# Gate weights of a second feed-forward: high part by a rounding DMA, low part by an accumulating DMA

## The chip, the cores and the metric

One core of one Trainium2 chip runs the whole program. The metric is the device time of one execution in microseconds (us); the kernel before takes 1485.97 us (median of three runs, 1485.88 to 1487.15).

## What is computed

Two layers of a transformer-like backbone over 512 latent and 128 context tokens, width 1024. Layer 0 has neighbourhood attention, layer 1 a bidirectional gated linear recurrence; each is followed by a feed-forward with SwiGLU, inner width 2816, and a final norm closes the network. The change lies in the second feed-forward:

```python
def _swiglu(x, w_gu, w_down):
    gate, up = jnp.split(x @ w_gu, 2, axis=-1)
    return (jax.nn.silu(gate) * up) @ w_down

f_c = _swiglu(_modulate(ctx, norm_g[i, 1], sh2_c, sc2_c), ffn_w_gu[i], ffn_w_down[i])
f_l = _swiglu(_modulate(lat, norm_g[i, 1], sh2_l, sc2_l), ffn_w_gu[i], ffn_w_down[i])
```

All in float32. The gate and up weights of one layer are 1024 x 2816 each.

## The kernel before, in words

Every matmul product is made of three passes in a reduced float32 format (`F32R` in the code): a value is split into a rounded high part and the remainder, the low part, and the product is high x high + high x low + low x high. So each weight tile (128 x 1024, 512 KB) has to become two tiles before TensorE can use it. `split` (L1527 to L1530) does that for a tile in `raw`: ScalarE copies it with rounding into the high part (L1529), VectorE subtracts the high part from `raw` into the low part (L1530).

The 2816 inner features are 22 tiles of 128. The second feed-forward (`ffn_halves`) handles them in chunks of 3, 3, 4, 4, 4 and 4; after each chunk a down projection (`project_part`, at the end `project_last`) adds the chunk's share to the tokens `x`. Tiles 0 to 2 are prepared in `opening`, the function ahead of it. For tiles 3 to 21, one call of `gate_weights` each (19 calls), a scheme with sums of blocks saves matmuls: the gate tile's two halves are the blocks A11 and A12, four sums S1 to S4 of gate and up blocks are formed by GpSimd (`sum_weights`, `s_sums`, L1175) and split in turn (`s_split`), and the second half of the up tile is split by `last_weights`. A tile's products run in three parts: `pair_a` (A11 and A12, L1203 to L1205 in `product`), `pair_b` (S2, S1, S3) and `pair_c` (A22, S4). Only `pair_a` reads the gate tile's high and low part; GpSimd's sums read the unsplit gate tile in `raw` as well.

Buffers: `raw` has three, filled by SP's DMA queue; `whi` and `wlo`, the high and low parts, have three each, shared in turn by the gate tiles and the weights of the down projection. The accumulator bank `mc` is one, reused by each tile. A scheduler in the build sets the order of each engine's instructions from its own estimate of times. Each engine then works strictly in that order, and an instruction that waits holds up all behind it.

The main lines are: in `gate_weights`, the DMA into `raw` (L1156), the two buffers and `self.split(hi, lo, raw)` (L1159).

Of the kernel before, what the change touches and what calls it, by code (L numbers as in the profile page):

```python
# [9 lines left out]
F32 = mybir.dt.float32  # L10
F32R = mybir.dt.float32r
AF = mybir.ActivationFunctionType
ALU = mybir.AluOpType
# [125 lines left out]
class _Step:  # L139
# [66 lines left out]
    def keep(self, todo, n):  # L206
        nc = self.nc
        for _ in range(min(n, len(todo))):
            name, f = key = todo.pop(0)
            raw = self.t([P, D], F32, "mraw", 3, self.sb)  # L210
            if name == "wg":
                nc.gpsimd.dma_start(raw.rearrange("p (f m) -> p f m", f=2), self.i[name][2 * f:2 * f + 2].rearrange("f p w d m -> p f (w d m)"))
            else:
                nc.gpsimd.dma_start(raw.rearrange("p (k m) -> p k m", k=KT), self.i[name][1, f] if name == "gu" else self.i[name][f])
            self.kept[key] = d = self.dram.tile([P, 2 * D], F32, tag=f"k{name}{f}", name=f"k{name}{f}")
            high, low = [self.t([P, D], F32R, n, 1, self.sb) for n in ("kwh", "kwl")]
            with self.tc.issue_after(self.mark[0]), self.tc.issue_after(self.mark[1]):
                nc.scalar.copy(high, raw)  # L218
                nc.vector.tensor_tensor(low, raw, high.bitcast(F32), ALU.subtract)
            for h, w in enumerate((high, low)):  # L220
                nc.gpsimd.dma_start(d[:, h * D:h * D + D], w.bitcast(F32))

    def two(self, src, x):
        nc = self.nc
        n = src.shape[2]
        raw = self.t([P, 2, n, P], F32, "raw", 3)
        nc.sync.dma_start(raw, src.rearrange("f p k m -> p f k m"))
        hi = self.t([P, 2, n, P], F32R, "whx" if x else "whi", 3, self.sb if x else None)
        lo = self.t([P, 2, n, P], F32R, "wlx" if x else "wlo", 3, self.sb if x else None)
        self.split(hi, lo, raw)  # L230
        return [(hi[:, j], lo[:, j]) for j in range(2)]
# [921 lines left out]
    def gate_weights(self, l, f):  # L1153
        nc = self.nc
        raw = self.t([P, KT, P], F32, "raw", 3)
        nc.sync.dma_start(raw, self.i["gu"][l, f])  # L1156
        hi = self.t([P, KT, P], F32R, "whi", 3)
        lo = self.t([P, KT, P], F32R, "wlo", 3)
        self.split(hi, lo, raw)  # L1159
        W = {n: (hi[:, a:a + KH], lo[:, a:a + KH]) for n, a in (("A11", 0), ("A12", KH))}  # L1160
        return {"W": W, "g": raw, "u": self.i["gu"][l, NF + f]}

# [517 lines left out]
```

## Time and profile before

| what | value |
|---|---|
| median of three runs | 1485.97 us (1485.88 to 1487.15) |
| the profiled execution | 1488.96 us, span 1487.1 us |
| TensorE matmul busy | 1471.2 us, 99% of the span |
| VectorE busy | 1075.0 us, 72% |
| ScalarE busy | 728.3 us, 49% |
| GpSimd busy | 247.9 us, 17% |
| second feed-forward, `gate_weights` on | about 1050 to 1480 us |

Engines are named PE (TensorE matmul), PEld (its weight loads), DVE (VectorE), ACT (ScalarE), POOL (GpSimd) and SP (the queue that issues most DMAs). A busy share is an average; what an engine waits for is read from its waits, stretch by stretch. Durations are those of one profiled execution.

### The profile page before, as it was taken

To read this page: it belongs to the slowest core of one execution; us is meant where nothing else is said; L and a number is where in the kernel's file an instruction comes from. 1 tells how busy PE (TensorE), PEld (TensorE's weight loads), DVE (VectorE), ACT (ScalarE), POOL (GpSimd) and SP (SyncE) were. 2 spreads that over 40 slices of the span, in tenths; PEclk is the share of its full clock that TensorE was granted. 3 is DMA by queue.
4 is the path that set the end of the run, shared out by engine and by line. 5 is a ranking of instruction groups with operands and counts; after the bars stand their busy time and mean duration, and the time that the engine had idled before them with its cause. 6 is when DMAs were issued, how large, how long until landed. Compare 5 with 4: busy or idle time off the path is not lost.

```text
span 1487.1 us, 26372 instructions
## 1 busy us (share of the span) xinstructions
PE 1471.2 (99%) x10377; PEld 1440.2 (97%) x10377; DVE 1075.0 (72%) x2054; ACT 728.3 (49%) x1345; POOL 247.9 (17%) x325
## 2 busy tenths in 40 slices
PE   9999999999999999999999999999999999999997
PEld 5999999999999999999999999999999999999997
DVE  6788887875678788887876489985865666565545
ACT  5676666754333234322434298864634343424344
POOL 0001000000012222211210001112032322222311
PEclk9999999999999999999999999999999999999999
DMA  9555555443359899886863744267242131313121
GB/s 371 179 151 172 170 151 155 126 157 100 114 177 323 299 358 326 305 264 218 306 221 125 252 142 142 86 236 247 81 132 86 57 114 57 114 57 109 52 68 71
DMA packets 86026, 255.35 MB, mean 172 GB/s; under 512 B 9056, under 2 KB 22544, under 8 KB 85776
## 3 DMA queue, kind: packets, MB, share of 16 engines
q1 hardware_dynamic: 59152, 157.06, 32.3%
q0 software_dynamic: 26576, 96.49, 18.8%
q8 instruction: 81, 1.33, 0.4%
q14 instruction: 41, 0.34, 0.1%
q10 hardware_dynamic: 176, 0.13, 0.0%
HBM read 206.18 MB, written 43.53 MB: 168 GB/s over the span
## 4 chain that ended last, share of the span: by engine, by line
PE 79%; DMA 8%; DVE 5%; issue 3%; ACT 3%; POOL 1%; DVEq 0%; ACTq 0%; POOLq 0%
PE mm L253 11%; PE mm L255 11%; PE mm L254 11%; PE mx L253 4%; PE mx L255 4%; PE mx L254 4%; PE mx L1203 3%; PE mx L1204 3%; PE mx L1205 3%; DMA mraw<-in_wm 2%; PE op L888 2%; PE gp L1412 2%; PE tp L806 2%; PE mc L1204 1%; PE mc L1203 1%
## 5 line engine op out<-in xcount | busy, mean ns | idle before, releaser
L253 PE MATMUL mm<-big,whi 128*128 128x320 f32 (+3 forms) x1010 | 311.0, 311 | 1.9 <-ACT big L1529 1.8
L254 PE MATMUL mm<-big,whi 128*128 128x320 f32 (+3 forms) x1010 | 312.7, 310 | 0.3 <-DVE big L1530 0.3
L255 PE MATMUL mm<-big,wlo 128*128 128x320 f32 (+3 forms) x1010 | 312.2, 310 | 0.0
L292 DVE SCALAR_TENSOR_TENSOR mprod<-mraw,csb 128x1024 f32<-128x1024 f32 x160 | 194.7, 1217 | 19.6 <-DMA mraw<-in_wm 19.4
L253 PEld LDWEIGHTS mm<-big,whi 128*128 128x128 f32 x1010 | 189.6, 189 | 4.0 <-ACT big L1529 2.4
L254 PEld LDWEIGHTS mm<-big,whi 128*128 128x128 f32 x1010 | 190.5, 189 | 1.7 <-DVE big L1530 0.5
L255 PEld LDWEIGHTS mm<-big,wlo 128*128 128x128 f32 x1010 | 190.1, 189 | 1.0
L1529 ACT CAST whi<-raw 128x1024 fp32r<-128x1024 f32 (+2 forms) x103 | 105.3, 1024 | 143.7 <-PE mm L254 89.6
L1530 DVE TENSOR_TENSOR wlo<-raw,whi 128x1024 fp32r<-128x1024 f32 (+2 forms) x103 | 127.4, 1238 | 33.4 <-ACT whi L1529 33.1
L254 PE MATMUL mm<-big,whx 128*128 128x320 f32 (+3 forms) x443 | 137.4, 310 | 0.0
L255 PE MATMUL mm<-big,wlx 128*128 128x320 f32 (+3 forms) x443 | 137.2, 310 | 0.0
L253 PE MATMUL mm<-big,whx 128*128 128x320 f32 (+3 forms) x443 | 137.0, 310 | 0.0
L595 DVE SCALAR_TENSOR_TENSOR x<-mm,G,x 128x320 f32<-128x320 f32 (+3 forms) x202 | 81.1, 435 | 55.9 <-PE mm L255 50.7
L253 PE MATMUL mx<-big,whi 128*128 128x320 f32 (+3 forms) x318 | 99.2, 312 | 0.0
L255 PE MATMUL mx<-big,wlo 128*128 128x320 f32 (+3 forms) x318 | 98.6, 310 | 0.0
L254 PE MATMUL mx<-big,whi 128*128 128x320 f32 (+3 forms) x318 | 98.4, 310 | 0.0
L288 POOL DMA_DIRECT2D mraw<-in_wm x80 | 42.9, 536 | 317.1 <-DVE mprod L292 203.9
L255 PEld LDWEIGHTS mm<-big,wlx 128*128 128x128 f32 x443 | 83.6, 189 | 0.0
L254 PEld LDWEIGHTS mm<-big,whx 128*128 128x128 f32 x443 | 83.5, 189 | 0.0
L253 PEld LDWEIGHTS mm<-big,whx 128*128 128x128 f32 x443 | 83.4, 188 | 0.0
L1530 DVE TENSOR_TENSOR wlx<-sum,whx 128x1024 fp32r<-128x1024 f32 x40 | 50.2, 1254 | 38.5 <-ACT whx L1529 38.5
L218 ACT CAST kwh<-mraw 128x1024 fp32r<-128x1024 f32 x33 | 34.7, 1051 | 75.6 <-DMA kwi<-kwh 27.7
(396 smaller groups left out, 3886.5 us busy)
## 6 DMA issues: line engine op xcount, KB each, us to landing
raw<-in_gu SPq DMA_DIRECT2D x84, 512.0 KB, 3.6
mraw<-in_wm POOLq DMA_DIRECT2D x80, 512.0 KB, 5.3
raw<-in_dn SPq DMA_DIRECT2D x24, 512.0 KB, 3.7
sw<-in_wm SPq DMA_DIRECT2D x16, 512.0 KB, 10.1
raw<-in_wqk SPq DMA_DIRECT2D x16, 512.0 KB, 4.4
mraw<-in_wi POOLq DMA_DIRECT2D x16, 512.0 KB, 6.4
kwi<-kwh POOLq DMA_DIRECT2D x16, 512.0 KB, 6.3
kwi<-kwl POOLq DMA_DIRECT2D x16, 512.0 KB, 5.4
```

Of the source, the lines that this page charges most:

```text
L218: nc.scalar.copy(high, raw)
L253: nc.tensor.matmul(ps, hi[:, k], xhi[:, k, s], start=(k == 0), stop=False)
L254: nc.tensor.matmul(ps, hi[:, k], xlo[:, k, s], start=False, stop=False)
L255: nc.tensor.matmul(ps, lo[:, k], xhi[:, k, s], start=False, stop=(k == nk - 1))
L288: nc.gpsimd.dma_start(w, self.i["wm"][l * 6 + j - 2, f])
L292: nc.vector.scalar_tensor_tensor(prod, w, 1.0, self.csb[:, s], ALU.mult, ALU.mult, accum_out=out[:, s, f:f + 1])
L595: last = self.nc.vector.scalar_tensor_tensor(xs, ps[:, a - t0:b - t0], G[:, s, f:f + 1], xs, ALU.mult, ALU.add).ins
L1203: nc.tensor.matmul(ps, hi[:, k], xh[:, k], start=start and k == 0, stop=False, skip_group_check=not start)
L1204: nc.tensor.matmul(ps, hi[:, k], xl[:, k], start=False, stop=False, skip_group_check=not start)
L1205: nc.tensor.matmul(ps, lo[:, k], xh[:, k], start=False, stop=(k == KH - 1), skip_group_check=not start)
L1529: high = self.nc.scalar.copy(hi, v).ins
L1530: return high, self.nc.vector.tensor_tensor(lo, v, hi.bitcast(F32), ALU.subtract).ins
```

## The change

A new function `rounded` takes the place of `split` in `gate_weights`. GpSimd's queue loads the gate tile once more from HBM, straight into the high part, rounding on the way; ScalarE writes the negated high part into the low part's buffer; a second GpSimd transfer adds the tile from HBM onto it, which leaves tile minus high part. The load into `raw` stays, since GpSimd's sums read it.

```diff
+    def rounded(self, hi, lo, src):
+        nc = self.nc
+        nc.gpsimd.dma_start(hi, src)
+        nc.scalar.mul(lo, hi.bitcast(F32), -1.0)
+        nc.gpsimd.dma_start(lo, src, accum_op=ALU.add)
...
     def gate_weights(self, l, f):
         nc = self.nc
         raw = self.t([P, KT, P], F32, "raw", 3)
         nc.sync.dma_start(raw, self.i["gu"][l, f])
         hi = self.t([P, KT, P], F32R, "whi", 3)
         lo = self.t([P, KT, P], F32R, "wlo", 3)
-        self.split(hi, lo, raw)
+        self.rounded(hi, lo, self.i["gu"][l, f])
```

Below, lines of the changed kernel are 6 higher than before; the numbers behind names count buffers.

The scheduler moves the work around the new instructions. On GpSimd, at the chunk of tiles 10 to 13, before: the sums of tiles 12 (`sum_14219`, `sum_14220`) and 13 stand in one row (`raw` holds the unsplit tiles).

```order
L1175 TENSOR_TENSOR sum_14219<-raw_14217 128x512
L1175 TENSOR_TENSOR sum_14220<-raw_14180,raw_14217 128x512
L1175 TENSOR_TENSOR sum_14219<-sum_14219,raw_14180 128x512
L1175 TENSOR_TENSOR sum_14220<-raw_14180,sum_14219 128x512
L1175 TENSOR_TENSOR sum_14352<-raw_14350 128x512
L1175 TENSOR_TENSOR sum_14352<-sum_14352,raw_14313 128x512
```

The same place on GpSimd in the changed kernel; the gate tiles 11 to 14 are `whi_14057`, `whi_14191`, `whi_14325` and `whi_14459`, their low parts one number higher.

```order
L1181 TENSOR_TENSOR sum_14230<-raw_14189,raw_14227 128x512
L225 DMA whi_14057<-in_gu 128x1024
L1181 TENSOR_TENSOR sum_14229<-sum_14229,raw_14189 128x512
L1181 TENSOR_TENSOR sum_14230<-raw_14189,sum_14229 128x512
L227 DMA wlo_14058<-in_gu 128x1024
L225 DMA whi_14191<-in_gu 128x1024
L227 DMA wlo_14192<-in_gu 128x1024
L225 DMA whi_14325<-in_gu 128x1024
L225 DMA whi_14459<-in_gu 128x1024
L227 DMA wlo_14326<-in_gu 128x1024
L227 DMA wlo_14460<-in_gu 128x1024
L1181 TENSOR_TENSOR sum_14363<-raw_14361 128x512
```

Between the sums of tile 12 and those of tile 13 now stand eight transfers of four tiles; the accumulate of tile 13 stands behind the load of tile 14.

On ScalarE, at the same chunk, before: the casts of tiles 11, 12 and 13 (`whi_14049`, `whi_14182`, `whi_14315`) and, behind them, that of tile 12's sums (`whx_14225`).

```order
L1529 CAST whi_14049<-raw_14047 128x1024
L1529 CAST whi_14182<-raw_14180 128x1024
L1529 CAST whi_14315<-raw_14313 128x1024
L1209 COPY snap_14066<-mx_14053 128x320
L1216 ACTIVATE g_14081<-g_14081 128x320
L1529 CAST wuh_14133<-raw_14084 128x512
L1529 CAST big_11721<-g_13692 128x320
L1529 CAST whx_14225<-sum_14219 128x1024
```

In the changed kernel (tile 12's sums are `sum_14229` here), the negations stand where the casts stood.

```order
L226 ACTIVATE wlo_14058<-whi_14057 128x1024
L226 ACTIVATE wlo_14192<-whi_14191 128x1024
L1215 COPY snap_14075<-mx_14062 128x320
L226 ACTIVATE wlo_14326<-whi_14325 128x1024
L1222 ACTIVATE g_14090<-g_14090 128x320
L1535 CAST wuh_14142<-raw_14093 128x512
L1535 CAST big_11721<-g_13700 128x320
L1535 CAST whx_14235<-sum_14229 128x1024
```

The negation of tile 13, which waits for a transfer into `whi_14325`, stands four rows ahead of the cast of tile 12's sums.

On TensorE, at tile 4 (`whi_12654`, `wlo_12655`), before: its first products in `pair_a`, and the down projection (`mm`) between them.

```order
L1203 MATMUL mx_12658<-big_11262,whi_12654 128x320
L1204 MATMUL mx_12658<-big_11262,whi_12654 128x320
L1205 MATMUL mx_12658<-big_11262,wlo_12655 128x320
L1203 MATMUL mx_12658<-big_11262,whi_12654 128x320
L1204 MATMUL mx_12658<-big_11262,whi_12654 128x320
```

In the changed kernel (tile 4 is `whi_12655` and `wlo_12656`):

```order
L1209 MATMUL mx_12660<-big_11262,whi_12655 128x320
L1210 MATMUL mx_12660<-big_11262,whi_12655 128x320
L259 MATMUL mm_12546<-big_11721,whi_12508 128x320
L260 MATMUL mm_12546<-big_11722,whi_12508 128x320
L261 MATMUL mm_12546<-big_11721,wlo_12509 128x320
L259 MATMUL mm_12546<-big_11721,whi_12508 128x320
```

The first product with the low part was the third matmul of the tile; now 27 matmuls of the down projection stand between the first two and it.

## Rows read from the trace of the kernel before

**Rows 1.** The page: busy us, share of the span and instructions of each engine.

```profile
PE 1471.2 (99%) x10377; PEld 1440.2 (97%) x10377; DVE 1075.0 (72%) x2054; ACT 728.3 (49%) x1345; POOL 247.9 (17%) x325
```

**Rows 2.** Busy us of each engine (instructions) by stretches, granted clock, DMA share.

```profile
core 0: us, PE busy (x) PEld busy (x) DVE busy (x) ACT busy (x) POOL busy (x), PEclk, DMA share, GB/s
1060.00:1080.00 20.00, 19.48 (x133) 19.22 (x132) 17.78 (x39) 11.47 (x25) 2.29 (x3) 1.00 0.38 124
1080.00:1130.00 50.00, 49.06 (x332) 48.57 (x332) 33.10 (x55) 19.93 (x32) 17.51 (x13) 1.00 0.33 99
1130.00:1180.00 50.00, 49.73 (x336) 49.23 (x335) 32.51 (x56) 19.18 (x30) 14.11 (x11) 1.00 0.31 95
1180.00:1230.00 50.00, 49.65 (x338) 49.38 (x337) 29.06 (x44) 24.16 (x41) 13.95 (x11) 1.00 0.28 85
1230.00:1280.00 50.00, 50.00 (x343) 50.00 (x342) 29.36 (x46) 16.20 (x27) 16.51 (x12) 1.00 0.21 64
1280.00:1330.00 50.00, 50.00 (x342) 50.00 (x341) 29.98 (x50) 17.79 (x26) 11.49 (x9) 1.00 0.32 96
1330.00:1380.00 50.00, 49.90 (x340) 49.64 (x339) 30.34 (x44) 23.14 (x40) 13.78 (x11) 1.00 0.31 95
1380.00:1430.00 50.00, 50.00 (x343) 50.00 (x342) 29.04 (x48) 17.27 (x26) 13.64 (x10) 1.00 0.24 70
1430.00:1487.00 57.00, 48.91 (x334) 47.81 (x332) 31.38 (x63) 25.42 (x51) 4.90 (x6) 0.96 0.17 60
sum 427.00, PE 416.73 PEld 413.84 DVE 262.55 ACT 174.56 POOL 108.17; mean PE 46.30 PEld 45.98 DVE 29.17 ACT 19.40 POOL 12.02
```

**Rows 3.** What TensorE waited for from 1000 us on: us in total, times, longest.

```profile
PE mx L1203 <- ACT snap L1209: 1.4, 3, 0.5
PE at L521 <- ACT snap L665: 0.4, 1, 0.4
PE mm L1203 <- DVE x L595: 0.4, 1, 0.4
PE mm L253 <- ACT big L1529: 0.4, 1, 0.4
PE mx L542 <- DVE dg L538: 0.3, 1, 0.3
```

**Rows 4.** Splitting weight tiles from 1000 us on: count, duration ns min/median/max.

```profile
L1529 ACT CAST whi<-raw x41: 824/1048/1056, 1060.0 to 1431.3; 128x1024 fp32r<-128x1024 f32 x33, 128x768 fp32r<-128x768 f32 x8
L1530 DVE TENSOR_TENSOR wlo<-raw,whi x41: 943/1225/2285, 1061.3 to 1432.4; 128x1024 fp32r<-128x1024 f32 x33, 128x768 fp32r<-128x768 f32 x8
```

**Rows 5.** GpSimd's loads into tile mraw, whole span: issue ns, then landings.

```profile
L288 POOL DMA_DIRECT2D mraw<-in_wm x80: 528/531/727, 45.1 to 752.9; - x80
...
L214 POOL DMA_DIRECT2D mraw<-in_wi x16: 527/536/563, 426.8 to 591.5; - x16
...
DMA to landing us min/median/max: 3.7/5.6/9.6
```

**Rows 6.** SP's queue from 1050 to 1440 us: packets, MB, share of 16 engines.

```profile
q1 hardware_dynamic: 12864, 33.03, 27.7%
```

**Rows 7.** The page: mean busy share of the DMA engines, in 40 slices, tenths.

```profile
DMA  9555555443359899886863744267242131313121
```

**Rows 8.** One of GpSimd's four sums of a tile, from 1050 to 1440 us.

```profile
L1175 POOL TENSOR_TENSOR sum<-raw x19: 1287/1295/1640, 1048.8 to 1414.7; 128x512 f32<-128x512 f32 x19
```

**Rows 9.** What SP's queue waited for from 1050 to 1440 us: total, times, longest.

```profile
SPq L1156 <- DVE wlo L1530: 103.3, 15, 13.7
SPq L227 <- POOL sum L1175: 46.6, 6, 10.3
```

## The prediction

> **What bounds the kernel now.** I read the page's busy line first: the matmul engine is busy 99% of the span, VectorE 72%, GpSimd 17% [rows 1]. That share is an average, so the table by stretches came next, for the second feed-forward's products and the stretch that closes it. TensorE is idle there for 0.52, 0.94, 0.27, 0.35, 0, 0, 0.10 and 0 us between 1060 and 1430 us, 2.2 us in all, at a granted clock of 1.00; VectorE and ScalarE are free a third to two thirds of the time [rows 2]. Last, TensorE's list of waits from 1000 us on: 2.9 us in seven waits, none for a weight tile's high or low part, none for a DMA [rows 3]. So TensorE bounds this stage, and the work that the change takes off VectorE is hidden today. The stretch 1280 to 1330 gives the pace: 342 matmuls in 50.00 us, 0.146 us each [rows 2].
>
> **The change part by part.** *Removed:* 19 gate tiles (feed-forward tiles 3 to 21) lose a subtraction of 1.225 us on VectorE [rows 4], 23.3 us of busy time that no TensorE wait is put down to [rows 3]: on the path 0, at most the 2.2 us above. *Exchanged:* the 19 rounding casts on ScalarE become 19 negations of the same 128x1024. No negation of that size is in the trace; the cast took 1.048 us [rows 4] and I take 1.05. *Added:* 38 transfers of 512 KB on GpSimd's queue. A load takes GpSimd 0.53 us to issue [rows 5]: 38 x 0.53 = 20 us beside its 108 us in 427 [rows 2], which is hidden as work. DMA traffic: the SP queue moved 33.03 MB in 390 us for 27.7% of the engines [rows 6], so 512 KB occupy all sixteen for 0.277 x 390 x 0.524 / 33.03 = 1.7 us. The additions are 19 x (1.7 + 3.4) = 97 us of 390: room enough on average.
>
> What matters is the chain from the release of a weight buffer to the low part's arrival. Before, it was cast and subtraction, 1.05 + 1.23 = 2.3 us [rows 4], on data that already lay in `raw`. Now it is rounding load, negation, accumulating transfer, one after the other. The trace has neither kind of transfer. Plain loads of this size on GpSimd's queue landed in 3.7 us at the least, 5.6 in the median and 9.6 at the most [rows 5]; these are the bounds for both. For the rounding load I take 4.0, near the low end, because the stage's DMA share is 0.21 to 0.38 [rows 2] where most of those loads ran at 5 to 9 tenths [rows 7]. The accumulating one reads the tile twice, from HBM and from its destination, so I give it one share more: 4.0 + 1.7 = 5.7. The Trainium skill says the same in "Collectives: The Full Stack", section "The bandwidth ceiling: the fold count and why AG ≠ RS ≠ AR": an add in the DMA path costs through its two source reads, about half the copy rate; by a plain copy's price the sum below would be near 0, by that rule what it is now. No run here shows it yet. With 0.3 us for three hand-overs (my allowance) the chain is 4.0 + 1.05 + 5.7 + 0.3 = 11.0 us, 8.7 longer than before.
>
> Against it stands the distance, in the changed order, from the last matmul that reads the buffer's previous content to the first that reads the new low part, at 0.146 us a matmul.
> - *Tiles 4, 5, 6* (TensorE rows of the change section): 72, 75 and 79 matmuls, 10.5, 11.0 and 11.5 us. Loads 5 and 6 stand on GpSimd right behind the accumulate of the tile before and share the DMA engines with it; of its two shares I charge one, 1.7 us. Waits 0.5 + 1.7 + 1.2 = 3.4 us.
> - *Tiles 8, 9:* tile 8's accumulate stands on GpSimd behind tile 9's load, which waits for its buffer and behind two sums of 1.3 us [rows 8]; tile 9's first product comes 39 matmuls, 5.7 us, after its buffer is free, and 4.0 + 1.7 are needed before any of that. I charge 3.
> - *Tiles 11 to 21 but the last of each four:* 104 to 107 matmuls, 15.2 us or more, so the low part itself arrives in time. But ScalarE's negation of the third tile (13, 17, 21) waits for a landing at the head of its queue (ScalarE rows): behind it stands the cast of the second tile's sums, behind that on VectorE a subtraction and the gate addition that frees the `mc` bank. From the release of the second tile's buffer to TensorE's product into that bank are 120 matmuls, 17.5 us. The chain: load 4.0 + 1.7, negation 1.05, two issues 1.1, third load behind a whole accumulate 4.0 + 3.4, negation 1.05, cast 1.05, subtraction 1.23, addition 0.5, hand-overs 0.4 = 19.5. So 2.0 us, three times: 6.
> - *The end:* the gate transfers delay GpSimd's sums, the sums free `raw` buffers, and SP's loads for the down projections already wait for such sums, 46.6 us in 6 waits [rows 9]. For the last projection I charge two waits of ScalarE's casts, 3 us.
>
> Sum: 3.4 + 3 + 6 + 3 = 15.4, rounded to 16 because GpSimd's queue also delays what I did not count. Against the profiled execution's own 1488.96 us (span 1487.1 and 1.9 around it) that is 1505; the median of the three runs lies 3.0 below that execution, so the forecast for the median is **1502 us**.
>
> Each further us on a tile's chain adds about 9 us (three tiles, two, three heads, the end), and from 2.5 us on the other ten tiles join. With the slowest landing for the accumulate, 9.6, this is 16 + 9 x 3.9 + 10 x 1.4 = 65 us: 1551. With both at 3.7 the chain is 8.8 and fits all tiles, and the head's chain (one share of sharing each) falls to 15.5 against 17.5: 0 us.
>
> **The rivals.** *Hidden after all (not slower).* The accumulate costs no more than the fastest plain load: it decides at 3.7 + 1.05 + 3.7 = 8.5 us against the shortest distance, 10.5. For it: the fastest landings, and the quiet DMA of this stage. Against it: tile 9's 5.7 us and the second read. Time 1486 to 1489, 17%.
> *Both transfers dear.* Rounding or accumulating slows the DMA engines themselves, or GpSimd's descriptors come late. For it: the median landing of 5.6, 1.9 over the least [rows 5]. Against: the issues took 531 and 536 ns in the median [rows 5], hardly varying beside a VectorE that was busy 72% [rows 1]. Then 1.6 us more on each of both transfers: 9 x 3.2 + 10 x 0.7 = 36 on top, 1538; at the slow end 1551 or more. 32%. The Trainium skill has a cause for it in "SBUF — State Buffer", section "Who interferes with whom": VectorE can lock GpSimd out of the port that it needs to generate descriptors, so GpSimd's DMAs start late. The issue rows show no such stretch.
> *VectorE's relief shows.* Subtractions gone, `raw` is freed earlier (SP waited 103.3 us in 15 waits for just these [rows 9]) and the loads come earlier. But TensorE has only 2.2 us to give back: 1484, which is 0.15%, inside the bound. Faster by more needs the tail too: 4%.
> *The rounding transfer only copies.* Then the low parts are zero and the precision is lost, but every transfer and wait is the same: no other time.
>
> **How the numbers follow.** No change means within 0.2%, 3 us, about what this measurement can tell: 1483 to 1489. The forecast case (1489 to 1520) has 47%, dear transfers 32%, hidden 17%, relief 4%. So faster 0.04, same 0.17, slower 0.79. The likeliest case alone is 1490 to 1520. The range for 8 in 10 takes in the hidden case at 1486 and the dear one to the slow-landing bound, 1555; a third of the dear case and most of the relief lie outside, some 15%.
>
> **What would show it.** After the change the page should have 38 more GpSimd DMAs, 19 fewer subtractions into `wlo`, and 19 `wlo` rows on ScalarE. TensorE's waits should name the landing of `wlo` at tiles 4 to 6, by 0.5 to 2 us each, and VectorE at the three heads by about 2; the clock should stay at 1.00. A landing of the accumulate near 5.7 proves the price, near 4 the hidden case, above 8 the dear one. I am wrong in mechanism if TensorE's new waits are not on these tiles, or if the stage's idle time is small while the time grows.

## The result, and the profile after

The changed kernel takes 1508.05 us (median of four runs, 1502.78 to 1508.57) against 1486.14 for the kernel before on the same chip. The ratio is 1.0137, with an interval of 1.012 to 1.0155: slower, by 18 to 23 us. The forecast was 1502. The profiled execution took 1507.81 us (span 1506.0), 18.9 us of span more than that of before.

The page's line of busy times after the change; it answers to [rows 1].

```profile
PE 1474.5 (98%) x10377; PEld 1439.9 (96%) x10377; DVE 1047.3 (70%) x2035; ACT 729.7 (48%) x1345; POOL 268.8 (18%) x363
```

VectorE lost 19 instructions and 28 us, GpSimd gained 38 and 21 us, ScalarE's count is the same: the work moved as planned, and no engine is near its limit but TensorE. Where the time went is in the stretches of the second feed-forward; the columns are those of [rows 2].

```profile
1080.00:1130.00 50.00, 46.18 (x310) 45.39 (x309) 28.81 (x50) 18.99 (x29) 19.12 (x17) 1.00 0.56 154
1130.00:1180.00 50.00, 48.21 (x323) 47.19 (x321) 29.14 (x54) 17.94 (x29) 17.67 (x16) 1.00 0.47 128
1180.00:1230.00 50.00, 47.49 (x321) 47.23 (x322) 23.87 (x39) 23.41 (x40) 12.70 (x14) 1.00 0.55 143
1230.00:1280.00 50.00, 48.16 (x318) 47.90 (x317) 19.61 (x39) 14.06 (x22) 19.89 (x19) 0.97 0.50 126
```

TensorE is idle 1.8 to 3.8 us in these stretches, where it was idle 0 to 0.9 before, and the DMA share, 0.21 to 0.33 there, is 0.47 to 0.56 now. TensorE's list of waits from 1060 us on (in total, times, longest) says for whom; `snap` is ScalarE's copy of a finished accumulator bank:

```profile
PE mx L1211 <- DMA wlo<-in_gu: 7.1, 5, 2.1
PE mc L1209 <- DVE g L1220: 6.2, 3, 2.7
PE mx L1209 <- ACT snap L1215: 2.4, 4, 1.2
PE mm L259 <- ACT whi L1535: 0.6, 1, 0.6
```

Against 2.9 us of waits before [rows 3] there are 17.8 now (with four small ones that are not shown): 14.9 more. The first row is that of the low parts, at five tiles: three waits of 2.1, 1.2 and 1.0 us between 1105 and 1135 us, where tiles 4, 5 and 6 stand, and two with 2.8 between 1170 and 1195, at tiles 7 and 8 (in brackets the idle time ahead and what ended it):

```profile
1181.21 0.42 PE L1211 MATMUL mx<-big,wlo 128*128 128x320 f32 x1 [1.49 <-DMA wlo<-in_gu]
1190.42 0.42 PE L1211 MATMUL mx<-big,wlo 128*128 128x320 f32 x1 [1.30 <-DMA wlo<-in_gu]
```

These end with the fifth and the sixth accumulate, those of tiles 7 and 8, which landed at 1181.2 and 1190.4. That of tile 9 landed at 1194.6, before TensorE's first product with it at 1195.2, so tile 9 did not wait; where expectations below speak of waits at tiles 8 and 9, they mean these two.

The second row of the list is the accumulator bank at three heads, the places where an instruction that waits for tile 13, 17 or 21 stands first in an engine's queue: 1.8, 1.7 and 2.7 us at 1267, 1349 and 1429.

The landings that stand behind both, by the two lines of the added transfers (issue ns min/median/max, then us to landing):

```profile
L225 POOL DMA_DIRECT2D whi<-in_gu x19: 556/606/857, 1060.4 to 1422.0; - x19
...
DMA to landing us min/median/max: 3.7/6.0/8.5
```

```profile
L227 POOL DMA_DIRECT2D wlo<-in_gu x19: 844/862/903, 1065.7 to 1429.6; - x19
...
DMA to landing us min/median/max: 5.2/5.5/8.3
```

The rounding load takes 3.7 us when it is alone; issued right behind an accumulating one it takes 6.0 to 8.5. The accumulate takes 5.2 at the least and 5.5 mostly, but 8.3, 6.5 and 7.9 at tiles 7, 8 and 9.

How a head stops TensorE is seen on two engines at tile 13. ScalarE first (start, duration, operation, and in brackets the idle time ahead and what ended it):

```profile
1265.82 1.06 ACT L226 ACTIVATE wlo<-whi 128x1024 fp32r<-128x1024 f32 x1 [6.37 <-DMA whi<-in_gu]
1266.78 0.46 ACT L1222 ACTIVATE g<-g 128x320 f32<-128x320 f32 x1
1267.14 0.60 ACT L1535 CAST wuh<-raw 128x512 fp32r<-128x512 f32 x1
```

VectorE at the same place:

```profile
1267.78 0.69 DVE L1536 TENSOR_TENSOR wul<-raw,wuh 128x512 fp32r<-128x512 f32 x1 [5.48 <-ACT wuh L1535]
1268.39 0.48 DVE L1536 TENSOR_TENSOR big<-g,big 128x320 fp32r<-128x320 f32 x1
1268.79 0.48 DVE L1220 TENSOR_TENSOR g<-mc,snap 128x320 f32<-128x320 f32 x1
```

ScalarE stood still 6.4 us for the landing of tile 13's high part, with the cast `wuh` of an up tile two places behind it; VectorE stood still 5.5 us for that cast; the addition that reads bank `mc` was VectorE's third instruction after that, at 1268.8, and TensorE's next product into the bank at 1269.3, 1.8 us late.

### The profile page after: what moved, and what is told of

It reads as the page before. It is cut to its first block, busy times and chain, and to the rows that moved or that the text cites. A ratio compares the mean times of both kernels' runs of the same rounds, so it can differ in the third digit from the quotient of the medians.

```text
span 1506.0 us, 26429 instructions
## 1 busy us (share of the span) xinstructions
PE 1474.5 (98%) x10377; PEld 1439.9 (96%) x10377; DVE 1047.3 (70%) x2035; ACT 729.7 (48%) x1345; POOL 268.8 (18%) x363
## 4 chain that ended last, share of the span: by engine, by line
PE 61%; DMA 16%; DVE 8%; issue 6%; POOL 4%; ACT 4%; SPq 0%; DVEq 0%; POOLq 0%; ACTq 0%
PE mm L259 9%; PE mm L261 9%; PE mm L260 9%; PE mx L259 3%; PE mx L260 3%; PE mx L261 3%; POOL sum L1181 3%; DMA mraw<-in_wm 2%; DMA raw<-in_gu 2%; PE op L894 2%; DMA whi<-in_gu 2%; DMA sw<-in_wm 2%; PE gp L1418 2%; PE tp L812 2%; DMA raw<-in_dn 2%
## 5 line engine op out<-in xcount | busy, mean ns | idle before, releaser
L1535 ACT CAST whi<-raw 128x1024 fp32r<-128x1024 f32 (+2 forms) x84 | 85.6, 1021 | 76.4 <-PE mm L260 42.4
L1536 DVE TENSOR_TENSOR wlo<-raw,whi 128x1024 fp32r<-128x1024 f32 (+2 forms) x84 | 99.7, 1187 | 29.7 <-ACT whi L1535 28.1
L226 ACT ACTIVATE wlo<-whi 128x1024 fp32r<-128x1024 f32 x19 | 20.2, 1061 | 109.3 <-DMA whi<-in_gu 102.6
```

The costliest lines, as they stand in the source:

```text
L1535: high = self.nc.scalar.copy(hi, v).ins
L1536: return high, self.nc.vector.tensor_tensor(lo, v, hi.bitcast(F32), ALU.subtract).ins
```

## The experiments

All but one of these kernels let the scheduler lay out the engines' orders anew, so a time alone can mislead; each is read together with its waits. Only the third has, row for row, the order of the changed kernel. Its kernel before is measured beside each group.

**1. The rounding transfer alone.** The low part is subtracted by VectorE again.

```diff
         nc.gpsimd.dma_start(hi, src)
-        nc.scalar.mul(lo, hi.bitcast(F32), -1.0)
-        nc.gpsimd.dma_start(lo, src, accum_op=ALU.add)
+        nc.vector.tensor_tensor(lo, raw, hi.bitcast(F32), ALU.subtract)
```

> The high part comes by the rounding transfer as in the change; the low part is VectorE's subtraction from `raw` as before, so the negation and the accumulating transfer are gone. Chain theory (what costs is the time from the release of a weight buffer to the arrival of its low part): the chain is a rounding transfer, 3.7 us alone in the trace of the change, plus the subtraction of 1.2, some 5.5 with hand-overs, well under the 10.5 us that the closest tiles have. TensorE's waits for a low part (7.1 us in 5) and for the accumulator bank mc (6.2 in 3) vanish: 1486 to 1489 us. Traffic theory (the doubled DMA traffic and GpSimd's issues delay SP's loads and the sums, and that is what costs): half of the added transfers remain, so about half of the 22 us: 1496 or more.

Measured: 1486.77 us against 1487.13, ratio 0.9991 (0.998 to 1.0003): no difference. The longest of TensorE's waits from 1060 us on, then the rounding loads, issue ns and us to landing:

```profile
PE mc L1209 <- DVE big L1042: 1.3, 1, 1.3
PE mx L1208 <- ACT snap L1214: 1.0, 2, 0.5
```

```profile
L225 POOL DMA_DIRECT2D whi<-in_gu x19: 537/577/606, 1058.8 to 1405.8; - x19
...
DMA to landing us min/median/max: 3.6/3.8/5.9
```

No wait is for a low part. The one for `mc`, at 1077 us, ends with a row of `opening`; between 1100 and 1450 us TensorE waits 1.0 us in all. So rounding in the transfer costs nothing beside a plain load (3.7 at the least in [rows 5]), half of the added traffic is free here, and what is dear is in the second half of the change.

**2. The accumulate alone.** The high part is cast by ScalarE again.

```diff
-        nc.gpsimd.dma_start(hi, src)
+        nc.scalar.copy(hi, raw)
         nc.scalar.mul(lo, hi.bitcast(F32), -1.0)
         nc.gpsimd.dma_start(lo, src, accum_op=ALU.add)
```

> The high part is ScalarE's cast from `raw` as before; the low part is made as in the change, by ScalarE's negation and the accumulating transfer. ScalarE has 19 instructions of 1.05 us more than in either kernel. Chain theory: cast 1.05 + negation 1.06 + accumulate 5.4 + hand-overs 0.5 = 8.0 us, under 10.5; and ScalarE no longer waits for a transfer ahead of its other work, so the three waits for the bank mc go too: 1486 to 1491 us, the waits for a low part under 2 us in sum. Rival, the accumulate itself (what costs is that a low part arrives by an accumulating transfer on GpSimd, whatever stands ahead of it): the waits for a low part stay near 7 us: 1497 or more. Traffic theory: half of the added transfers remain: about 1497.

Measured: 1493.33 us, ratio 1.0044 (1.0028 to 1.006), between the two forecasts. From TensorE's waits in its trace:

```profile
PE mx L1211 <- DMA wlo<-in_gu: 5.6, 5, 1.8
```

The waits for `mc` are gone, as the chain theory said, but five waits for a low part remain, and at other tiles: 3, 5, 10, 14 and 18. Tile 14 shows one of them (the others are not followed here), in the order of time on ScalarE:

```profile
1273.05 1.05 ACT L225 CAST whi<-raw 128x1024 fp32r<-128x1024 f32 x1 [1.05 <-DMA raw<-in_gu]
1274.01 1.04 ACT L1535 CAST whx<-sum 128x1024 fp32r<-128x1024 f32 x1
1274.95 1.06 ACT L226 ACTIVATE wlo<-whi 128x1024 fp32r<-128x1024 f32 x1
```

Here the chain begins not with the release of the weight buffer but with `raw`, which lands late; the accumulate was issued at 1276.3 and landed 5.3 us later. In the kernel before a cast and a subtraction followed, 2.3 us, and fitted.

**3. No addition.** The second transfer overwrites. Every engine's order is that of the change.

```diff
-        nc.gpsimd.dma_start(lo, src, accum_op=ALU.add)
+        nc.gpsimd.dma_start(lo, src)
```

> As the change, but the second transfer overwrites instead of adding, so the low part holds the rounded weight again and not the remainder. Both transfers, the negation and every wait stay. It prices the addition. Chain theory: the second transfer lands in about 3.7 us where the accumulate took 5.25 to 5.5 alone, so each chain is 1.7 us shorter and the two transfers share less: the five waits for a low part fall from 7.1 to about 1 us, those for mc from 6.2 to about 3 (one of the transfers that the third negation of a chunk waits behind is shorter): 1494 us, 1490 to 1498. Rival, the second hop and not the addition costs: a plain load of that size takes 5 or more here too, and it stays at 1503 or more.

Measured: 1492.85 us, ratio 1.0039 (1.0024 to 1.0054), inside the forecast. TensorE's waits from 1060 us on, then the landings of the second transfer:

```profile
PE mx L1211 <- DMA wlo<-in_gu: 2.7, 2, 2.4
PE mx L1209 <- ACT snap L1215: 2.5, 5, 1.1
PE mc L1209 <- DVE g L1220: 0.6, 1, 0.6
```

```profile
L227 POOL DMA_DIRECT2D wlo<-in_gu x19: 537/538/580, 1070.2 to 1420.2; - x19
...
DMA to landing us min/median/max: 3.7/3.9/5.4
```

This is the price of the word "add", with nothing else changed: 3.7 to 3.9 us to landing instead of 5.2 to 5.5, 0.54 us of issue instead of 0.86, and the rounding loads beside it land in 4.6 in the median instead of 6.0. It is worth some 15 us of the 22. The waits for low parts and `mc` fell from 13.3 to 3.3 us.

**4. The heads' negations late.** At tiles 13, 17 and 21 the negation stands behind the casts of the previous tile's sums on ScalarE.

```diff
-        nc.scalar.mul(lo, hi.bitcast(F32), -1.0)
+        with self.tc.issue_after(self.cast) if late else nullcontext():
+            nc.scalar.mul(lo, hi.bitcast(F32), -1.0)
```

> As the change, but the negations of tiles 13, 17 and 21 may only stand on ScalarE behind the casts of the previous tile's sums. Nothing is computed or moved by DMA differently. Chain theory: the three waits for the bank mc (6.2 us, and 1.9 us of lower clock behind the first of them) come from ScalarE waiting for the landing of these tiles' high parts with those casts behind it; they go, and the waits for a low part at tiles 4, 5, 6, 8 and 9 stay at 7 us: 1508 - 8 = 1500 us, 1498 to 1502. Rival, late sums (the bank is freed late since GpSimd's sums come late behind the transfers): the waits stay, 1506 or more.

Measured: 1499.2 us, ratio 1.0081 (1.0064 to 1.0098), as forecast. From TensorE's waits:

```profile
PE mx L1212 <- DMA wlo<-in_gu: 5.9, 6, 2.2
PE mm L260 <- ACT whi L1536: 3.0, 2, 1.7
```

No wait for `mc` is left. A new row took its place: the down projection waits for its weights' casts, 3.0 us in two.

**5. A longer chain.** ScalarE copies, then negates in place.

```diff
-        nc.scalar.mul(lo, hi.bitcast(F32), -1.0)
+        nc.scalar.copy(lo, hi.bitcast(F32))
+        nc.scalar.mul(lo, lo.bitcast(F32), -1.0)
```

> As the change, but ScalarE makes the negated high part in two instructions (a copy, then a negation in place), so each chain is 1.06 us longer; result and transfers are the same. Chain theory: the waits at tiles 4, 5, 6, 8 and 9 grow by 1.06 us each, 5.3 in sum, and the three waits for the bank mc by one to two such instructions, 3 to 6: 1508 + 8 to 11 = 1517, 1514 to 1521. Rival, traffic or late sums: 20 us more of work on a ScalarE that is busy less than half of the time costs nothing: 1506 to 1510.

Measured: 1507.67 us (1502.36 to 1516.8), ratio 1.0148 (1.0121 to 1.0175): the change's time, where 1514 to 1521 were expected. The low parts' waits did grow, from 7.1 in 5 to 9.5 in 8, but those for `mc` fell from 6.2 to 1.5, by TensorE's waits:

```profile
PE mx L1212 <- DMA wlo<-in_gu: 9.5, 8, 2.2
...
PE mc L1210 <- DVE g L1221: 1.5, 2, 1.1
```

The two instructions were placed apart, with other work between them, so the heads were laid out differently. As a measure of what a microsecond on the chain costs the run decides nothing.

**6. The traffic alone.** The kernel before, and the same transfers into HBM that nothing reads.

```diff
+        dum = self.dram.tile([P, 2 * D], F32, tag=f"dum{f}", name=f"dum{f}")[:, 0:D]
+        src = self.i["gu"][l, f].rearrange("p k m -> p (k m)")
+        with self.tc.issue_after(self.sum or self.next):
+            nc.gpsimd.dma_start(dum, src)
+            nc.gpsimd.dma_start(dum, src, accum_op=ALU.add)
         self.split(hi, lo, raw)
```

> The kernel before, and beside it on GpSimd's queue, after the sums of the tile before, the same 38 transfers of 512 KB as in the change (19 loads, each followed by an accumulating one), but into memory that nothing reads: HBM to HBM, not into a weight buffer. GpSimd waits for each load before it issues its accumulating one, as in the change. Chain theory: no wait for a low part or for mc, since nothing waits for these transfers; 1486 to 1491 us (the sums behind a waiting GpSimd come up to 5 us late). Traffic theory: the time of the change, 1500 or more.

Measured: 1509.05 us, ratio 1.0149 (1.0135 to 1.0162). The chain theory's number is missed by 18 us. But the time is lost at another place: nothing waits for a low part or `mc`; TensorE waits 12.2 us in 6 for ScalarE's `snap`, which stands behind a cast that waits for a down-projection load. The row of TensorE's waits, and the longest case in the order of time on ScalarE:

```profile
PE mx L1212 <- ACT snap L1218: 12.2, 6, 3.9
```

```profile
1148.15 0.83 ACT L1538 CAST whi<-raw 128x768 fp32r<-128x768 f32 x1 [4.61 <-DMA raw<-in_dn]
1148.89 0.42 ACT L1218 COPY snap<-mx 128x320 f32<-128x320 f32 x1
```

The loads by size and their median us to landing, in 1050 to 1450 us of this run and then in 1050 to 1470 us of the change:

```profile
raw<-in_dn SPq DMA_DIRECT2D x15, 512.0 KB, 4.5
raw<-in_dn SPq DMA_DIRECT2D x8, 384.0 KB, 6.0
```

```profile
raw<-in_dn SPq DMA_DIRECT2D x16, 512.0 KB, 3.5
raw<-in_dn SPq DMA_DIRECT2D x8, 384.0 KB, 3.4
```

The dummies, placed behind the sums, meet the down projection's loads and slow them. Beside the waits, TensorE's clock was at the lower level in three stretches of this stage, 13.6 us together, which costs half of that, 6.8 us. In the change these loads land as fast as before (3.6 and 3.5 us there). So the run shows that such traffic is not free wherever it stands, and that it is not what happened in the change.

**7 and 8. Halves.** Load, negation and accumulate each in two halves of 256 KB; in 8 with the late negation of run 4 as well.

```diff
+        for a in (0, KH):
+            s = slice(a, a + KH)
+            nc.gpsimd.dma_start(hi[:, s], src[:, s])
+            nc.scalar.mul(lo[:, s], hi[:, s].bitcast(F32), -1.0)
+            nc.gpsimd.dma_start(lo[:, s], src[:, s], accum_op=ALU.add)
```

> As the change, with all three steps in two halves of 256 KB (A11, then A12): load, negation and accumulate of the first half do not wait for the second. GpSimd issues 76 transfers instead of 38. A transfer of 512 KB lands in 3.7 us, of which the engines' own share is about 1.7 by the working of the prediction, so a half should land in about 2.9 and a half accumulate in about 4.0 to 4.5. Chain theory: the first half's chain is 2.9 + 0.55 + 4.3 + 0.5 = 8.3 us instead of 10.5 to 12, the second half is needed 12 matmuls (1.75 us) later and comes about that much later: the five waits for a low part (7.1 us) fall to 2 or less, those for mc (6.2) shrink by about a us each: 1498 us, 1493 to 1502. Rival, GpSimd's issue time (0.55 and 0.86 us an issue, doubled): no gain or a loss, 1506 or more.

> The halves of the run before, and the negations of tiles 13, 17 and 21 behind the casts of the previous tile's sums on ScalarE. Chain theory: both groups of waits are reached: 1493 us, 1489 to 1496. If halving gains nothing, it equals the late negation alone, 1499.

Measured: 1518.42 us, ratio 1.0205 (1.0188 to 1.0223), and 1504.95, ratio 1.0113 (1.0098 to 1.0128). In run 7 the rival was right: halves cost 10 us against the change. In run 8 they cost 6 against run 4, which neither forecast had. TensorE's waits for a low part did fall in run 7, from 7.1 us to 4.7, but those for `mc` rose from 6.2 to 7.0, those for `snap` from 2.4 to 7.9, and 2.8 for a high part are new. The lines of the two transfers in run 7 (issue ns and us to landing):

```profile
L227 POOL DMA_DIRECT2D whi<-in_gu x38: 537/845/1228, 1059.5 to 1432.2; - x38
...
DMA to landing us min/median/max: 2.9/6.3/8.0
```

```profile
L229 POOL DMA_DIRECT2D wlo<-in_gu x38: 859/890/1898, 1063.7 to 1439.7; - x38
...
DMA to landing us min/median/max: 3.8/5.3/8.5
```

A half alone lands in 2.9 us, as estimated, but an accumulate costs GpSimd 0.86 us or more to issue whatever its size, and the second half queues behind the first: the median landing of a half load, 6.3, is that of a whole one. That this queue is the whole loss is argued from these rows; no run changes the issue time alone.

**9. The change where the distance is long.** Tiles 3 to 10 as in run 1, tiles 11 to 21 as in run 4.

```diff
         nc.gpsimd.dma_start(hi, src)
+        if f < 11:
+            nc.vector.tensor_tensor(lo, raw, hi.bitcast(F32), ALU.subtract)
+            return
```

> Tiles 3 to 10, where the distance is short, take the rounding transfer and VectorE's subtraction (the first experiment's way); tiles 11 to 21, with 104 matmuls of distance or more, take the change's way with the late negation of tiles 13, 17 and 21. 11 of the 19 accumulating transfers stay. Chain theory: the waits for a low part at the short tiles (5.9 us in the late negation's run) and those for mc are gone; what is left are the waits of that run for the casts of the down projection's weights behind the late negations, 3.0 us: 1490 us, 1487 to 1493. Rival, the accumulating transfers cost by their number or their traffic: 11/19 of the change's 22 us: 1499.

Measured: 1496.39 us (1492.0 to 1501.01), ratio 1.0064 (1.0047 to 1.008), 3 above the range. The waits are as the chain theory said; TensorE's, then the first case on ScalarE:

```profile
PE mm L263 <- ACT whi L1539: 3.6, 3, 1.8
```

```profile
1289.29 1.04 ACT L1539 CAST whi<-raw 128x1024 fp32r<-128x1024 f32 x1 [3.45 <-DMA raw<-in_dn]
```

No low part, no `mc`. The reason that the expectation gave for the remaining wait was wrong, though: the cast waits for a load, and the load for a buffer that a late sum of GpSimd frees. SP issued it at 1285.7, right behind the last of tile 14's sums (1284.4 to 1285.7); before it was issued at 1280.2. Late sums are a real cost, the one that the prediction charged at the end alone. The waits from 1060 us on are 3.3 us more than before, not 10; the six executions, at mean clocks of 0.992 to 0.999, spread over 9 us, and two of them took 1492.0 and 1492.6. The profiled one took 1498.12, with a span 9.1 us longer than before. Of these, 2.8 lie ahead of the changed stage: the 7300th of the 10377 matmuls, the same one in both kernels, starts at 1026.4 us and not at 1023.6. Another 1.7 are a stretch at the lower clock at 1290. What the other executions lost is not known.

**10. The traffic without GpSimd's wait.** As run 6, each accumulate onto the block loaded a tile earlier.

```diff
-            nc.gpsimd.dma_start(dum, src, accum_op=ALU.add)
+            if self.dum is not None:
+                nc.gpsimd.dma_start(self.dum, src, accum_op=ALU.add)
+        self.dum = dum
```

> The dummy transfers of the traffic run again, but each accumulating one goes onto the block of HBM that was loaded a tile earlier, so GpSimd does not wait for a landing between the two (37 transfers instead of 38). Theory of the waiting GpSimd: without its 76 us of waits the sums and the loads come as before and most of that run's 22 us go: 1487 to 1493. Theory of collision: the loads of the down projection (4.5 and 6.0 us to landing in that run against 3.6 and 3.5 before) are slowed by the dummies' own traffic at that place, and casts wait for them: it stays at 1500 or more.

Measured: 1504.85 us, ratio 1.012 (1.0105 to 1.0135). GpSimd's waits for its own loads fell from 76.0 us to 3.2, yet the down projection's loads still took 4.5 and 6.0 us. TensorE waited 6.5 us in 4 for casts of their weights and 5.5 in 5 for `snap`. So collision is most of what these two runs paid for; the waiting GpSimd is worth at most the 4 us between them.

**11. The negation on VectorE.**

```diff
-        nc.scalar.mul(lo, hi.bitcast(F32), -1.0)
+        nc.vector.tensor_scalar(lo, hi.bitcast(F32), -1.0, None, ALU.mult)
```

> As the change, but VectorE makes the negation. ScalarE then waits for no transfer at all. Chain theory: the low parts' waits stay near 7 us (VectorE's negation takes about as long); the three waits for mc stay too, since the additions that free the bank stand on VectorE behind the waiting negation: 1505 us, 1500 to 1511. Rival, ScalarE's own load is what fails at the heads: the mc waits go: 1499 or less.

Measured: 1505.9 us, ratio 1.0115 (1.01 to 1.0129), as forecast: low parts 6.6 us in 5, `mc` 3.2 in 3. The waits for `mc` are shorter than the change's 6.2; the negation takes 0.69 us on VectorE, not 1.06. But all three stay, so it is not ScalarE's load: whichever engine waits for the landing holds up what stands behind it.

**12. Eight accumulates, no forced order.** Tiles 11, 12, 14, 15, 16, 18, 19 and 20 as in the change, the others as in run 1.

```diff
+        if f < 11 or f in (13, 17, 21):
+            nc.vector.tensor_tensor(lo, raw, hi.bitcast(F32), ALU.subtract)
+            return
```

> All 19 high parts by the rounding transfer; the low parts by negation and accumulating transfer at the eight tiles 11, 12, 14, 15, 16, 18, 19 and 20 alone, by VectorE's subtraction at the tiles with a short distance (3 to 10) and at the heads (13, 17, 21). No order is forced. Chain theory: at these eight the low part has 104 matmuls, 15 us, against a chain of 10.5 to 12, and no head waits behind them on ScalarE, so eight accumulating transfers cost nothing: 1486 to 1490 us, no wait for a low part, and for mc 1 us at most. Rival, each accumulating transfer costs its share (22 us / 19) wherever it stands: 1495 or more.

Measured: 1500.12 us (1494.58 to 1506.34), ratio 1.0097 (1.0079 to 1.0116): the chain theory's time is missed by 10. It is the rival's time, but not by the rival's way. TensorE's waits, then VectorE in the order of time at tile 13:

```profile
PE mc L1212 <- DVE g L1223: 6.6, 3, 2.6
...
PE mx L1214 <- DMA wlo<-in_gu: 0.2, 1, 0.2
```

```profile
1255.57 1.23 DVE L227 TENSOR_TENSOR wlo<-raw,whi 128x1024 fp32r<-128x1024 f32 x1 [8.48 <-issue]
```

Half of the theory held: the eight low parts cost 0.2 us. But the heads did not go away with the accumulate of tile 13. Its rounding load still stands on GpSimd behind tile 12's accumulate; it was issued at 1248.7 and landed at 1255.5, and now VectorE stands idle ahead of the same additions, 8.5 us. The view names no releaser, but the subtraction starts 0.1 us after that landing. So the head is a matter of the third tile's high part, not of its low part, and I had put the remedy at the wrong transfer. Run 2, where ScalarE casts that part, had no such wait.

## Why the prediction was right

The time came out 6 us above the forecast and inside its range, by the mechanism that it named: low parts that come after TensorE wants them, and heads that hold up the accumulator bank. That the sum of the waits agrees to 0.3 us is in part luck, since the terms for single tiles do not.

- *Removed work is hidden:* right as far as it was tested. No wait of TensorE before is put down to a subtraction into `wlo` [rows 3], and VectorE's 28 us less brought nothing visible. Run 1, which keeps the subtractions and takes the 19 casts off ScalarE, ties. No run takes the subtractions off without the longer chain.
- *The prices.* Rounding load 4.0 alone and 5.7 beside an accumulate: 3.7 at the least, 5.0 at tile 4, and 6.0 to 8.5 right behind an accumulate. Negation 1.05: 1.06 in the rows. Accumulate 5.7: 5.2 to 5.5 mostly, 8.3 at the most. Run 7 allows a check of the reason that was given: a half lands 0.8 us earlier than a whole for a load (2.9 and 3.7 at the least), 1.4 earlier for an accumulate (3.8 and 5.2). So the share that goes with the bytes is, by this estimate, 1.6 us of a whole load and 2.8 of a whole accumulate, 1.75 times as much; another 0.3 is the accumulate's longer issue. The Trainium skill has the rule in "Collectives: The Full Stack", section "The bandwidth ceiling: the fold count and why AG ≠ RS ≠ AR", for a ReduceScatter between cores: its add is slower since it needs two source reads. The 1.75 here comes near it. By time, too, the addition is dear: at the same order run 3 takes 1493 without it, the change 1508 with it.
- *Tiles 4, 5, 6:* forecast 0.5, 1.7 and 1.2, in all 3.4; measured 2.1, 1.2 and 1.0, in all 4.3. At tile 4 the load took 5.0 us and not 4.0, and its accumulate stood 0.9 us behind one of GpSimd's sums, which no term held.
- *Tiles 8, 9:* forecast 3; measured 1.3 at tile 8 and nothing at tile 9. Tile 7, for which the prediction put nothing and gave no reason, waited 1.5: tile 8's load was issued 1.0 us after the accumulate of tile 7, and the two took 8.5 and 8.3 us to land. Tile 8 did not wait by the way that was told, its accumulate behind tile 9's load: that load was issued at 1180.0, and GpSimd then stood idle 3.3 us, until tile 8's own late load had landed and been negated. So 2.8 against 3 is luck.
- *Heads:* 2.0 each, 6 in all; measured 1.8, 1.7 and 2.7, 6.2 in all. The way was ScalarE to VectorE to the bank as told, but by other members: the cast `wuh` of an up tile with its subtraction, not the cast of the second tile's sums. From the issue of the second tile's load (the release of its buffer does not show) to the product into the bank 18.2, 18.0 and 19.2 us went by, where the chain was put at 19.5; less the wait these are 16.3 to 16.5, where the distance was put at 17.5. The chain came out 0.3 to 1.5 us shorter and the distance 1.0 to 1.2, which nearly cancels. Run 4 removed just these three waits, run 11 kept them on another engine.
- *The end:* forecast 3, measured 1.8 (1.2 for a `snap` and 0.6 for a cast, both in 1440 to 1460 us). Runs 4 and 9 show such late loads at the ends of other chunks; that in the change the heads' waits hide them there is likely but not shown.
- *Sum:* 15.4 forecast, 15.1 in these waits. The 6 us of the miss lie elsewhere. The step from the profiled execution to the median took 3.0 off; that failed, since the profile of the change (1507.81) stands at its median, while that of before stood 3.0 above its own. The other 2.9 are the span: 18.9 longer and not 16. All of TensorE's waits together are 14.9 us more than before; of the 4.0 that are not waits, 1.7 are a stretch at a lower clock, below, which no term held. Nearly all of the other 2.3 lies at the edges of the waits. At 1350.6, where 1.71 us idle are listed, 2.01 lie between the starts of the two matmuls around the wait and 0.26 to the next start, where 0.146 is usual: 0.27 more than listed. There are 17 waits after and 7 before, so this is an estimated 2.7 us.
- *The rivals.* "Hidden" failed at the accumulate's price, 5.2 and not 3.7. Even at 3.7 (run 3) 3.3 us of these waits were still there, 2.4 of them at tile 5, where the load took 6.4 us and the second transfer stood 1.4 behind GpSimd's sums. "Dear transfers" failed as a rule: the issue rows are steady, 844 to 903 ns for an accumulate, and the median landing is 5.5. At tiles 7 to 9 landings did come to the dear price, 6.5 to 8.3. "Relief" had at most the 2.2 us to give back, and no run has it alone.
- *What was weaker than it sounded:* "about 9 us for each further us on a chain" stays untested. Run 3, at the same order, takes 15 us off for 1.5 us on the accumulate and 1.4 on the loads beside it, but that is the way down, where waits end at nothing; run 5, with a new order, paid nothing for its 1.06 us; an unchanged order with a longer chain was not tried. "Room enough on average" for the DMA traffic held only by its place: runs 6 and 10 lose 18 to 22 us to as many bytes at another place, written to HBM there. Two readings were off without consequence: VectorE is busy 17.8 of the 20 us from 1060 on [rows 2], not free for a third; and the head's chain of 15.5 at two transfers of 3.7 has one share of sharing in all, with one for each load it is 17.2, still below 17.5.

A version faster than before was not found, and TensorE has only 2.2 us to give in this stage; run 1 ties. More buffers for the high and low parts, the plain remedy for a longer chain, were not tried.

## What to carry to other kernels

Before work is moved from an idle engine into DMAs, count the chain from the release of the buffer to its last write, and hold it against the matmuls that lie between, tile by tile, with what stands ahead of each transfer in the queue that issues it: a subtraction of 1.2 us that nothing waits for is cheaper than a transfer of 5.4 us that something does. An instruction that waits for a transfer at the head of an engine's queue delays what stands behind it, so look for a reader of an accumulator bank there. And where a scheduler lays out the order, an edit is read by its waits first and its time second.

## What was not expected of the hardware

After one wait at a head TensorE's granted clock fell. The stretches around it, of the change (columns as in [rows 2]):

```profile
1265.00:1270.00 5.00, 3.16 (x21) 2.90 (x21) 2.22 (x4) 4.18 (x7) 0.88 (x1) 1.00 0.61 156
1270.00:1275.00 5.00, 5.00 (x26) 5.00 (x25) 2.61 (x4) 2.44 (x6) 1.46 (x2) 0.66 1.02 239
1275.00:1280.00 5.00, 5.00 (x36) 5.00 (x35) 1.15 (x3) 1.30 (x4) 4.46 (x4) 1.00 0.21 40
```

TensorE was idle 1.8 us at 1267.5; in the 5 us from 1270 on the mean granted clock was 0.66, which is the lower of its two levels, 1.2 GHz, for 3.4 us and costs 1.7, and then 1.00 again. No stretch of this stage showed that before [rows 2] ahead of the last one. The wait of 2.7 us at 1429 in the same execution was not followed by such a fall, so a wait's length alone does not say it. The profiles of run 1 and of runs 5 to 12 show one to three such falls in this stage too, each begun during or soon after a wait (the shortest 1.2 us, the longest 4.8); those of runs 2, 3 and 4 and of the kernel before show none there. The kernels with waits are less steady, and a lower mean clock goes with a longer time. The six executions of run 12, time and mean clock: 1494.58 at 0.998, 1498.05 at 0.997, 1498.07 at 0.996, 1502.45 at 0.995, 1502.17 at 0.993, 1506.34 at 0.992. From 0.998 to 0.992 is an estimated 9 us in 1500, most of the 11.8 between the first and the last. The kernel before, eleven times beside it, stayed at 0.996 to 0.999 and within 5 us. That an accumulate costs GpSimd 0.86 us to issue, against 0.54 for a load, whatever its size, was not expected either.
